# Time mixing: small products on 64x64 tiles, and TensorE's order pinned as written

## The chip, the cores and the metric

The kernel runs on one core of one Trainium2 chip. A core has five engines with a queue each: TensorE (PE, matrix products into PSUM), VectorE (DVE), ScalarE (ACT), GpSimd (POOL) and SyncE (SP, which issues the loads here). The metric is the device time of one execution in microseconds. Three runs of the kernel before took 2772.35, 2776.08 and 2783.49 us; the median is 2776.08.

## The reference

A trunk of two layers over 256 positions of width 2048, in f32. The first layer is RWKV-7 time mixing with 32 heads of 64, followed by a squared-ReLU MLP; the second is banded attention and an MLP. The part that matters is the recurrence of the time mixing:

```python
kk = heads(k * k_k)
kk = kk / jnp.maximum(jnp.sqrt(jnp.sum(kk * kk, axis=-1, keepdims=True)), 1e-12)
k = k * (1 + (a - 1) * k_a)
decay = jnp.exp(-jnp.exp(heads(w_log)))

def step(S, inp):
    r_t, w_t, k_t, v_t, kk_t, a_t = inp
    sa = jnp.einsum('bhvk,bhk->bhv', S, -kk_t)
    S = (S * w_t[:, :, None, :] + sa[..., None] * (kk_t * a_t)[:, :, None, :]
         + v_t[..., None] * k_t[:, :, None, :])
    y = jnp.einsum('bhvk,bhk->bhv', S, r_t)
    return S, y
```

After it `y` is normalized per head, `sum(r*k*r_k)*v` is added, the result is multiplied by a gate `g` and goes through `w_o`.

## The kernel before

Everything is held transposed, channels on the 128 partitions and 256 positions along the row. Two heads fill the partitions, so the 2048 channels are 16 *pairs* (`Pair`). The recurrence is done in 4 chunks of 64 positions: inside a chunk the update by `sa` is a triangular system, which `invert` solves by inverting a 64x64 matrix per head and chunk, doubling the size of the inverted blocks level by level (1, 2, 4, 8, 16, 32).

A pair goes through four stages, which run as generators, one yield a step:

- the projections (`proj_steps` in `layer_a`): k and r of the pair, 2 x 16 units of *large* products. A unit (`proj2`, L394 and L395) multiplies 128 rows by the high half of the weights with 512 columns and by the low half with 256. The weights are split into the halves `wH` (ACT, L360) and `wL` (DVE, L363) in f32r. The generator yields every 2 units, 16 steps.
- `early` (8 steps): decay and learning rate from the LoRA products (L130, L131), the norm of `kk`, the scaled keys `kr`, `bh`, `kh`.
- `invert` (13 calls): the products `gr` of keys per chunk, then the inversion, which ends in `uf` (`u`).
- `late` (16 steps): the chain over chunks (`g`, `sa`, the state `zs`, and `py`, the output), three steps a chunk, then the norm of the output and the gate.

In round `p` of the loop (19 rounds) four pairs are under way: `late` of pair p-3, `invert` of p-2, `early` of p-1, the projections of p. A round has 16 slots. In each slot the three small stages go on by their share of steps, then the projections by one. From round 16 on, products of `w_o` (L383 to L385) stand in for the projections. In some slots one step of the adaLN sums is put in (`ada`: DVE adds a row of weights to `acc`, L423; `ada_sum` reduces `acc` on TensorE, L435).

The order of each engine's queue is chosen at compile time by a scheduler, which plays the program through with estimated durations and takes the earliest traced instruction that is ready. One thing is fixed by hand here: with `issue_after(other[-back])` (L817) the large products of a slot go behind the last small product of the slot before. Apart from that the scheduler may put large products ahead of small ones that aren't ready, and the reverse.

A product of f32 operands runs as two instructions (two passes), each with a weight load of its own. The instruction shapes differ by stage: `each` (L97) takes one 64x64 tile of TensorE per head; `tiles` (L103) works on the 32x32 diagonal or off-diagonal blocks of the inversion, four (two at the last level) side by side; `head_sums` (L120) sums the squares over each head with one 128x128 matrix `bones`, after `parts` (L106 to L116) has split the operand into two f32r halves on ACT and POOL; the large products take 128x128.

The inversion's level `l` in words: `u` holds the inverted 32x32 diagonal blocks, `tt` its 32x32 transposes (DVE, L235), `al` the masked blocks of the matrix (POOL, L239); first product `al`,`tt` into PSUM `iv`, copied to `xs` (ACT, L241); second product `xs`,`u`, added to `u` (DVE, L252). The last level joins the two 32-row halves with `co`, and `uf` collects the result.

Of the kernel before, what the change touches and what calls it, by code (L numbers as in the profile page):

```python
# [36 lines left out]
def _constants():  # L37
# [10 lines left out]
    put("cols", np.tile(np.array([RMS_EPS, GN_EPS, -0.5, 1.0, 1 / 32], np.float32), (P, 1)))  # L48
# [5 lines left out]
    for l in range(5):  # L54
        b = 1 << l
        m = ((i[:, None] // (2 * b) == i[None, :] // (2 * b))
             & (i[:, None] % (2 * b) >= b) & (i[None, :] % (2 * b) < b))
        put(f"lev{l}", np.tile(-m.T[:H, :H].astype(np.float32), (2, 1)))
    put("eye", np.eye(C))
    put("eye_h", np.tile(np.eye(H), (2, 1)))  # L60
    p = np.arange(P)
    bones = (p[:, None] // C == p[None, :] // C).astype(np.float32)
    put("bones", bones)
# [6 lines left out]
QS = [slice(H * i, H * i + H) for i in range(4)]  # L70
C_RMS, C_GN, C_MHALF, C_ONE, C_32ND = range(5)


class Pair:
# [19 lines left out]
    def each(self, o, lhsT, rhs):  # L94
        for c in range(4):
            for K in self.heads:
                self.b.nc.tensor.matmul(o(c)[K], lhsT(c)[K], rhs(c)[K], start=True, stop=True)  # L97

    def tiles(self, o, lhsT, rhs, pairs):

        for c in range(4):
            for R, K in pairs:
                self.b.nc.tensor.matmul(o[QS[K], c, :], lhsT[QS[R], c, :], rhs[QS[R], c, :], start=True, stop=True,  # L103
                                        tile_position=(H * R, H * K))

    def parts(self, func, src, scale=1.0):  # L106

        nc, pw = self.b.nc, self.b.pw
        H, L = (pw.tile([P, T], F32R, tag=n, bufs=2, name=n) for n in ("sH", "sL"))
        nc.scalar.activation(H, src, func, scale=scale)  # L110
        if func != AF.Copy:
            t = self.s("pt", 2)
            nc.scalar.activation(t, src, func, scale=scale)
            src = t
        nc.gpsimd.tensor_tensor(out=L, in0=src, in1=H, op=ALU.subtract)  # L115
        return H, L  # L116

    def head_sums(self, ps, parts):
        for i, t in enumerate(parts):
            self.b.nc.tensor.matmul(ps, self.b.bones, t, start=(i == 0), stop=(i == 1))  # L120

    def early(self):
# [7 lines left out]
        nc.tensor.matmul(z[:, 0:T], lw[:, 0, :], self.tw, start=True, stop=True)  # L130
        nc.tensor.matmul(z[:, T:2 * T], lw[:, 1, :], self.ta, start=True, stop=True)  # L131
# [7 lines left out]
        sq = self.parts(AF.Square, k, vec("k_k", j))  # L139
# [39 lines left out]
        rkp = self.parts(AF.Copy, rkp)  # L179
# [13 lines left out]
    def invert(self):  # L193
        b, nc, s, ch, kr, bk, bh, kh = self.b, self.b.nc, self.s, self.ch, self.kr, self.bk, self.bh, self.kh
        cst, pp = b.cst, b.pp

        def every(name):
            return cst(name).unsqueeze(1).to_broadcast([P, 4, H])

        def half(name, bufs):  # L200
            return b.pw.tile([P, 4, H], F32, tag=name, bufs=bufs, name=name)

# [11 lines left out]


        da, co, u = half("da", 2), half("co", 2), half("u", 2)
        for i, K in enumerate(QS):
            n = H * (i % 2)
            nc.scalar.copy(da[K], pg[K, :, n:n + H])
            if i % 2 == 0:  # L220
                nc.scalar.mul(co[K], pg[K, :, H:C], -1.0)
        nc.gpsimd.tensor_tensor(out=u, in0=da, in1=every("lev0"), op=ALU.mult)
        yield
        nc.vector.tensor_tensor(out=u, in0=u, in1=every("eye_h"), op=ALU.add)
# [6 lines left out]
        uf = self.u = b.uf[self.j % 2]  # L231
        down, up = ((0, 1), (2, 3)), ((1, 0), (3, 2))
        for l in range(1, 6):
            tt_, xs = half("tt", 1), half("xs", 1)
            nc.vector.transpose(out=tt_.rearrange("p c t -> p (c t)"), in_=u.rearrange("p c t -> p (c t)"))  # L235
            pi = pp.tile([P, 16, H], F32, tag="iv", bufs=1, name="iv")[:, 0:4, :]
            if l < 5:
                al = half("al", 2)
                nc.gpsimd.tensor_tensor(out=al, in0=da, in1=every(f"lev{l}"), op=ALU.mult)  # L239
                self.tiles(pi, al, tt_, [(i, i) for i in range(4)])  # L240
                nc.scalar.copy(xs, pi)  # L241
            else:
                self.tiles(pi, co, tt_, down)
                for i, K in enumerate(QS):
                    if i % 2:
                        nc.scalar.copy(xs[K], pi[K])
                    nc.gpsimd.tensor_copy(uf[K, :, H * (i % 2):H * (i % 2) + H], u[K])
            yield
            pi = pp.tile([P, 16, H], F32, tag="iv", bufs=1, name="iv")[:, 0:4, :]
            if l < 5:  # L250
                self.tiles(pi, xs, u, [(i, i) for i in range(4)])
                nc.vector.tensor_tensor(out=u, in0=u, in1=pi, op=ALU.add)  # L252
            else:
                self.tiles(pi, xs, u, up)
                for K in QS[::2]:
                    nc.vector.tensor_copy(uf[K, :, H:C], pi[K])
            if l == 2:
                pg = pp.tile([P, 4, P], F32, tag="gr", bufs=1, name="gr")
                self.each(lambda c: pg[:, c, :], lambda c: ch(kh)[:, c, :], lambda c: kr[:, c, :])
                mk = self.mk = self.big("mk", 2)  # L260
                nc.vector.tensor_tensor(out=mk, in0=pg, in1=ui, op=ALU.mult)
            yield

    def late(self):
# [7 lines left out]
        for c in range(4):  # L272
            pch = pp.tile([P, 3, C], F32, tag="chn", bufs=1, name="chn")
            g, sa = (pw.tile([P, C], F32, tag=n_, bufs=2, name=n_) for n_ in ("g", "sa"))
            for K in heads:
                nc.tensor.matmul(pch[K, 0, :], mk[K, c, 0:C], bk[K, 2, c, :], start=True, stop=(c == 0))  # L276
            if c:
                for K in heads:
                    nc.tensor.matmul(pch[K, 0, :], kr[K, c, 0:C], zs[K, :], start=False, stop=True)
            nc.scalar.copy(g, pch[:, 0, :])  # L280
            yield
            for K in heads:
                nc.tensor.matmul(pch[K, 1, :], u[K, c, :], g[K, :], start=True, stop=True)
            nc.scalar.mul(sa, pch[:, 1, :], -1.0)
            for K in heads:
                nc.tensor.matmul(ch(py)[K, c, :], bk[K, 2, c, :], mk[K, c, C:P], start=True, stop=False)
            if c:
                for K in heads:
                    nc.tensor.matmul(ch(py)[K, c, :], zs[K, :], kr[K, c, C:P], start=False, stop=False)
            yield  # L290
            if c < 3:
                for K in heads:
                    nc.tensor.matmul(pch[K, 2, :], bk[K, 1, c, :], bk[K, 2, c, :], start=True, stop=False)
                for K in heads:
                    nc.tensor.matmul(pch[K, 2, :], bk[K, 0, c, :], sa[K, :], start=False, stop=True)
# [7 lines left out]
            for K in heads:  # L303
                nc.tensor.matmul(ch(py)[K, c, :], sa[K, :], ch(ar)[K, c, :], start=False, stop=True)
# [3 lines left out]
        sq = self.parts(AF.Square, py)  # L308
# [8 lines left out]
        for i in range(2):  # L317
            nc.tensor.matmul(pg, self.lg[:, i, :], self.tg[:, i, :], start=(i == 0), stop=(i == 1))
# [5 lines left out]
class Body:  # L324
# [52 lines left out]
    def proj(self, ps, w, a, kts=(0, KT), first=True, last=True):  # L377

        nc = self.nc
        for kt in range(*kts):  # L380
            H, L = w[kt // HK]
            i = kt % HK
            nc.tensor.matmul(ps, H[:, i, :], a(kt)[:, 0, :], start=(first and kt == 0), stop=False)  # L383
            nc.tensor.matmul(ps, H[:, i, :], a(kt)[:, 1, :], start=False, stop=False)
            ins = nc.tensor.matmul(ps, L[:, i, :], a(kt)[:, 0, :], start=False, stop=(last and kt == KT - 1))  # L385
        return ins.ins

    def proj2(self, ps, w, a, kts=(0, KT)):

        nc = self.nc  # L390
        for kt in range(*kts):
            H, L = w[kt // HK]
            i = kt % HK
            nc.tensor.matmul(ps, H[:, i, :], a(kt), start=(kt == 0), stop=False)  # L394
            ins = nc.tensor.matmul(ps[:, 0, :], L[:, i, :], a(kt)[:, 0, :], start=False, stop=(kt == KT - 1))  # L395
# [34 lines left out]
    def ada_sum(self, acc, dst, half, bias):  # L430
        nc = self.nc
        ps = self.psm()[:, :HK]
        for n in range(HK):
            for g in range(0, P, 32):
                nc.tensor.matmul(ps[g:g + 32, n:n + 1], acc[:, n * P + g:n * P + g + 32], self.col(C_ONE),  # L435
# [19 lines left out]

    def last_pe(self):
        pe = self.nc.tensor.engine
        return next(i for i in reversed(self.nc.cur_bb.bb.instructions) if i.engine == pe)
# [61 lines left out]
    def run(self):  # L520
# [16 lines left out]
        self.lazy, self.fins = False, iter(())  # L537
        self.ada_done = set()
# [40 lines left out]
    def layer_a(self, st, sp):  # L579
# [169 lines left out]
        with ExitStack() as s1:  # L749
# [5 lines left out]
            self.bones = pw.tile([P, P], F32R, name="bones")  # L755
            self.uf = [pw.tile([P, 4, C], F32, name=f"uf_{i}") for i in range(2)]
            nc.scalar.copy(self.bones, self.cst("bones"))
            for e, u in zip(e01, self.uf):
# [69 lines left out]
            self.fin(HK)  # L828
        return v
# [261 lines left out]
```

## Time and profile before

| | |
|---|---|
| runs before | 2772.35, 2776.08, 2783.49 us |
| profiled execution | 2773.6 us |
| its span, granted clock | 2771.8 us, 0.986 |
| first `gr` product | 248.4 us |
| first and last start of `chn` (L276, L283) | 261.2, 752.4 us |
| first and last start of `o` (L383, L385) | 684.1, 780.5 us |

The time mixing's loop over pairs lies between some 222 us (first `pj` unit at 221.7) and 752 us of the span; what stands before it computes v and the adaLN values, what stands behind it is `w_o`, the MLPs and the attention. In rows of the profile, busy time is the union of an engine's instructions; matmuls overlap, so the time a matmul costs is read from one start to the next, not from its duration. A timeline row merges successive instructions of one line: start, length, engine, line, tiles, shape, count. In a row by groups the numbers behind the bar are busy time, the mean of one in ns, the engine's idle time before them and what ended it.

### The profile page before, as it was taken

The page shows a single profiled execution, that of the slowest core. Times are in us where ns is not written, and L with a number is a line of the kernel's source. Part 1 is how long each engine was busy: PE and PEld are TensorE (multiplying, and loading weights), DVE is VectorE, ACT ScalarE, POOL GpSimd, SP SyncE. Part 2 cuts the span into 40 slices and gives each one's busy share as a digit, 9 for nine tenths or more (in the row PEclk, how much of TensorE's full clock was granted, in tenths as well). Part 3 has the DMA queues.
Part 4 walks back from the last instruction along what each step waited for, and adds up shares of the span by engine and source line. Part 5 has one row for each costly group of instructions (what it writes and reads, how often), then busy time and mean ns, then how long its engine had stood idle before and what let it go on. Part 6 is the DMA issues. An engine that isn't in the chain of part 4 may idle for free.

```text
span 2771.8 us, 57644 instructions
## 1 busy us (share of the span) xinstructions
PE 2653.9 (96%) x23402; PEld 2217.6 (80%) x23402; DVE 2087.3 (75%) x3098; ACT 1260.9 (45%) x2214; POOL 301.8 (11%) x416
## 2 busy tenths in 40 slices
PE   6998999999998999999999899999989999999997
PEld 3677777777887888888888788877878888888886
DVE  4568778878889888888788896799786566665665
ACT  2345555556344434344344354465444344443444
POOL 0003443443220000000000200000100000000002
PEclk9999999999999999999999999999999999999999
DMA  9886556555687888888888868888876555555553
GB/s 297 269 281 193 169 171 196 176 176 162 216 302 243 298 308 305 300 314 296 299 306 302 304 218 282 268 293 268 279 242 216 187 186 186 187 183 189 185 188 122
DMA packets 217387, 662.60 MB, mean 239 GB/s; under 512 B 21408, under 2 KB 68896, under 8 KB 217120
## 3 DMA queue, kind: packets, MB, share of 16 engines
q1 hardware_dynamic: 215056, 656.36, 71.5%
q8 instruction: 184, 3.01, 0.4%
q10 hardware_dynamic: 2064, 2.54, 0.3%
q14 instruction: 83, 0.68, 0.1%
HBM read 656.72 MB, written 2.10 MB: 238 GB/s over the span
## 4 chain that ended last, share of the span: by engine, by line
PE 76%; DVE 9%; DMA 7%; issue 4%; POOL 1%; ACT 1%; DVEq 0%; SPq 0%; ACTq 0%; POOLq 0%
PE pj L394 40%; PE pj L395 20%; DMA raw<-w_ada 5%; DVE wL L363 3%; DVE acc L423 2%; PE iv L103 2%; PE gr L97 1%; DMA raw<-w_ada_kv 1%; PE m L625 1%; DVE un L504 1%; PE o L383 1%; PE ms L97 1%; POOL sL L115 1%; PE chn L276 1%; DVE aHL L506 1%
## 5 line engine op out<-in xcount | busy, mean ns | idle before, releaser
L394 PE MATMUL pj<-aHL,wH 128*128 128x512 f32 x3712 | 1353.5, 405 | 26.0 <-DVE aHL L506 22.4
L360 ACT CAST wH<-raw 128x1024 fp32r<-128x1024 f32 x772 | 807.0, 1047 | 949.4 <-PE pj L394 622.1
L363 DVE TENSOR_TENSOR wL<-raw,wH 128x1024 fp32r<-128x1024 f32 x772 | 946.1, 1228 | 290.7 <-ACT wH L360 288.8
L395 PE MATMUL pj<-aHL,wL 128*128 128x256 f32 x3712 | 1049.3, 283 | 7.5 <-DVE wL L363 7.2
L394 PEld LDWEIGHTS pj<-aHL,wH 128*128 128x128 f32 x3712 | 700.3, 189 | 199.2 <-issue 28.0
L394 PE MATMUL pj<-hHL,wH 128*128 128x512 f32 x2048 | 722.0, 397 | 4.5 <-DVE hHL L882 4.5
L395 PEld LDWEIGHTS pj<-aHL,wL 128*128 128x128 f32 x3712 | 705.3, 190 | 14.6 <-DVE wL L363 11.9
L395 PE MATMUL pj<-hHL,wL 128*128 128x256 f32 x2048 | 574.3, 281 | 4.6 <-DVE wL L363 4.5
L423 DVE SCALAR_TENSOR_TENSOR acc<-raw,ct,acc 128x1024 f32<-128x1024 f32 x360 | 470.4, 1307 | 139.8 <-DMA raw<-w_ada 104.0
L394 PEld LDWEIGHTS pj<-hHL,wH 128*128 128x128 f32 x2048 | 384.3, 188 | 97.9 <-DVE hHL L882 6.7
L395 PEld LDWEIGHTS pj<-hHL,wL 128*128 128x128 f32 x2048 | 386.8, 189 | 8.1 <-DVE wL L363 7.7
L482 POOL TENSOR_TENSOR ss<-ss,sq 128x256 f32<-128x256 f32 x56 | 65.0, 1160 | 1599.7 <-ACT sq L481 1599.4
L901 DVE SCALAR_TENSOR_TENSOR x<-pj,mod,x 128x256 f32<-128x256 f32 x256 | 123.1, 481 | 51.7 <-PE pj L395 48.8
L881 ACT CAST hHL<-t 128x256 fp32r<-128x256 f32 x128 | 51.4, 403 | 67.6 <-DVE t L880 67.3
L625 PE MATMUL m<-rawa,crep 128*32 128x256 f32 x512 | 47.4, 449 | 17.5 <-DMA rawa<-w_ada 16.9
L481 ACT ACTIVATE sq<-x 128x256 f32<-128x256 f32 x60 | 25.0, 418 | 70.5 <-DVE x L901 39.6
L880 DVE SCALAR_TENSOR_TENSOR t<-t 128x256 f32<-128x256 f32 x128 | 53.9, 422 | 3.0
L882 DVE TENSOR_TENSOR hHL<-t,hHL 128x256 fp32r<-128x256 f32 x128 | 53.4, 418 | 0.6 <-ACT hHL L881 0.5
L862 DVE TENSOR_TENSOR t<-pj,t 128x256 f32<-128x256 f32 x128 | 53.2, 417 | 0.0
L239 POOL TENSOR_TENSOR al<-da,csts 128x128 f32<-128x128 f32 x64 | 40.7, 647 | 67.4 <-PE iv L103 62.7
L861 ACT COPY t<-pj 128x256 f32<-128x256 f32 x128 | 46.6, 366 | 0.0
L685 PE MATMUL t<-aHL,wH 128*128 128x256 f32 x128 | 38.1, 298 | 5.8 <-DVE v L693 3.6
(230 smaller groups left out, 2483.0 us busy)
## 6 DMA issues: line engine op xcount, KB each, us to landing
raw<-w_ada SPq DMA_DIRECT2D x320, 512.0 KB, 4.7
raw<-w_up SPq DMA_DIRECT2D x256, 512.0 KB, 4.9
raw<-w_down SPq DMA_DIRECT2D x256, 512.0 KB, 4.3
rawa<-w_ada SPq DMA_DIRECT2D x64, 512.0 KB, 6.8
raw<-w_ada_kv SPq DMA_DIRECT2D x64, 512.0 KB, 5.4
raw<-w_k SPq DMA_DIRECT2D x32, 512.0 KB, 4.2
raw<-w_r SPq DMA_DIRECT2D x32, 512.0 KB, 4.7
raw<-w_o SPq DMA_DIRECT2D x32, 512.0 KB, 5.2
```

The costliest lines, as they stand in the source:

```text
L97: self.b.nc.tensor.matmul(o(c)[K], lhsT(c)[K], rhs(c)[K], start=True, stop=True)
L103: self.b.nc.tensor.matmul(o[QS[K], c, :], lhsT[QS[R], c, :], rhs[QS[R], c, :], start=True, stop=True, tile_position=(H * R, H * K))
L360: nc.scalar.copy(Hf, raw)
L363: eng.tensor_tensor(out=Lf, in0=raw, in1=Hf, op=ALU.subtract)
L394: nc.tensor.matmul(ps, H[:, i, :], a(kt), start=(kt == 0), stop=False)
L395: ins = nc.tensor.matmul(ps[:, 0, :], L[:, i, :], a(kt)[:, 0, :], start=False, stop=(kt == KT - 1))
L423: nc.vector.scalar_tensor_tensor(out=acc, in0=raw, scalar=ck, in1=acc, op0=ALU.mult, op1=ALU.add)
L482: (eng or nc.gpsimd).tensor_tensor(out=self.ss, in0=self.ss, in1=sq, op=ALU.add)
L625: nc.tensor.matmul(ps[g:g + 32, part, :W], crep[:, kt, :], raw[:, i, :], start=(part == 1 and kt < 4), stop=(part == 0 and kt >= KT - 4), ...
L880: nc.vector.scalar_tensor_tensor(out=t, in0=t, scalar=0.0, in1=t, op0=ALU.max, op1=ALU.mult)
L882: nc.vector.tensor_tensor(out=h[:, 1, :], in0=t, in1=h[:, 0, :], op=ALU.subtract)
L901: nc.vector.scalar_tensor_tensor(out=x, in0=ps[:, i, :], scalar=self.mods[(layer, 5)][:, n:n + 1], in1=x, op0=ALU.mult, op1=ALU.add)
```

## The change

Three things are changed, all in the pair loop.

1. `tiles` goes. The inversion's products use `each`, so one 64x64 tile per head: the masked matrix has 64 rows and 64 columns a chunk (`level`), the moving operand 32 columns (`tt` or `u`). `xs` is spread to 64 columns by two ACT copies with an even and an odd row mask as scale, and the last level uses two buffers `corner` with zeros in the other half. The first level, elementwise before, becomes a product with `eye_h`.
2. `parts` and `bones` go. `head_sums` takes f32 operands and one 64x64 tile per head.
3. `mm` wraps every product of the loop: while `in_order` is set, the instruction is put behind the one traced before it on TensorE. The loop runs the small stages in every slot and the projections, two steps (4 units), in every second slot; `fin(2)` in every slot becomes `fin(4)` in every second.

```diff
     def each(self, o, lhsT, rhs):
         for c in range(4):
             for K in self.heads:
-                self.b.nc.tensor.matmul(o(c)[K], lhsT(c)[K], rhs(c)[K], start=True, stop=True)
+                self.b.mm(o(c)[K], lhsT(c)[K], rhs(c)[K], start=True, stop=True)
...
+    def head_sums(self, ps, t):
+        for K in self.heads:
+            self.b.mm(ps[K], self.b.cst("ones")[K, 0:C], t[K], start=True, stop=True)
...
+        def level(l):
+            t = s("al", 2)
+            nc.gpsimd.tensor_tensor(out=ch(t), in0=ch(A), in1=cst(f"lev{l}").unsqueeze(1).to_broadcast([P, 4, C]),
+                                    op=ALU.mult)
+            return t
+
+        def product(lhsT, rhs):
+            pi = pp.tile([P, 16, H], F32, tag="iv", bufs=1, name="iv")[:, 0:4, :]
+            self.each(lambda c: pi[:, c, :], lambda c: ch(lhsT)[:, c, :], rhs)
+            return pi
...
+        A = s("da", 2)
+        nc.scalar.copy(ch(A), pg[:, :, 0:C])
+        al = level(0)
+        yield
+        pi = product(al, lambda c: cst("eye_h"))
+        tt = blocks("tt", 1)
+        nc.vector.tensor_tensor(out=tt, in0=pi, in1=eye_h, op=ALU.add)
+        u = turned(tt)
...
         for l in range(1, 6):
             if l < 5:
+                pi = product(level(l), lambda c: tt[:, c, :])
+                xs = s("xs", 1)
+                for i, own in enumerate((even, odd)):
+                    nc.scalar.activation(spread(xs)[:, :, i, :], pi, AF.Copy, scale=own)
...
             yield
+            pi = product(xs, lambda c: u[:, c, :])
             if l < 5:
                 nc.vector.tensor_tensor(out=u, in0=u, in1=pi, op=ALU.add)
+                tt = turned(u)
...
+    def mm(self, *args, **kw):
+        ins = self.nc.tensor.matmul(*args, **kw)
+        return self.tc.keep_in_program_order(ins) if self.in_order else ins
...
-            stages = ((Pair.late, 16), (Pair.invert, 13), (Pair.early, Pair.EARLY), (None, 16))
-            smalls, larges = [], []
+            stages = ((Pair.late, 16), (Pair.invert, 12), (Pair.early, Pair.EARLY), (None, 16))
+            self.in_order = True
...
-                    for gens, own, other, back in ((live, smalls, larges, 0), ([dense], larges, smalls, 2)):
-                        with tc.issue_after(other[-back]) if back and len(other) >= back else nullcontext():
-                            for g in gens:
-                                while g[2] * 16 < g[1] * (slot + 1):
-                                    next(g[0], None)
-                                    g[2] += 1
-                        own.append(self.last_pe())
+                    for g in live + ([dense] if slot % 2 else []):
+                        while g[2] * 16 < g[1] * (slot + 1):
+                            next(g[0], None)
+                            g[2] += 1
                     self.lazy = True
-                    self.fin(2)
+                    if slot % 2:
+                        self.fin(4)
```

More of the change, by code (lines that the diff above doesn't have):

```diff
@@ L1 @@
 import math
-from contextlib import ExitStack, nullcontext
+from contextlib import ExitStack
 import numpy as np
@@ L96, in each @@
             for K in self.heads:
[L97 to L120, printed above, removed]
+                self.b.mm(o(c)[K], lhsT(c)[K], rhs(c)[K], start=True, stop=True)
+    def head_sums(self, ps, t):
+        for K in self.heads:
+            self.b.mm(ps[K], self.b.cst("ones")[K, 0:C], t[K], start=True, stop=True)
     def early(self):
@@ L129, in early @@
         z = b.psm()
-        nc.tensor.matmul(z[:, 0:T], lw[:, 0, :], self.tw, start=True, stop=True)
-        nc.tensor.matmul(z[:, T:2 * T], lw[:, 1, :], self.ta, start=True, stop=True)
+        b.mm(z[:, 0:T], lw[:, 0, :], self.tw, start=True, stop=True)
+        b.mm(z[:, T:2 * T], lw[:, 1, :], self.ta, start=True, stop=True)
         sw, a = s(), s()
@@ L138, in early @@
         yield
-        sq = self.parts(AF.Square, k, vec("k_k", j))
+        sq = s()
+        nc.scalar.activation(sq, k, AF.Square, scale=vec("k_k", j))
         for o in (sw, a):
@@ L194, in invert, with blocks, spread, turned @@
         b, nc, s, ch, kr, bk, bh, kh = self.b, self.b.nc, self.s, self.ch, self.kr, self.bk, self.bh, self.kh
[L195 to L200, printed above, removed]
+        cst, pp, tt = b.cst, b.pp, None
+        def blocks(name, bufs):
             return b.pw.tile([P, 4, H], F32, tag=name, bufs=bufs, name=name)
+        def spread(t):
+            return t.rearrange("p (c i t) -> p c i t", c=4, i=2)
+        def level(l):
[7 more added lines that the diff above has]
+            return pi
+        def turned(t):
+            o = blocks("tt", 1) if t is not tt else blocks("u", 2)
+            nc.vector.transpose(out=o.rearrange("p c t -> p (c t)"), in_=t.rearrange("p c t -> p (c t)"))
+            return o
         ui = cst("ui").unsqueeze(1).to_broadcast([P, 4, P])
@@ L230, in invert @@
         yield
-        uf = self.u = b.uf[self.j % 2]
-        down, up = ((0, 1), (2, 3)), ((1, 0), (3, 2))
+        uf = self.u = s("uf", 2)
+        even, odd = b.col(C_EVEN), b.col(C_ODD)
         for l in range(1, 6):
-            tt_, xs = half("tt", 1), half("xs", 1)
-            nc.vector.transpose(out=tt_.rearrange("p c t -> p (c t)"), in_=u.rearrange("p c t -> p (c t)"))
-            pi = pp.tile([P, 16, H], F32, tag="iv", bufs=1, name="iv")[:, 0:4, :]
             if l < 5:
[L238 to L241, printed above, removed]
-            else:
[L243 to L247, printed above, removed]
+                pi = product(level(l), lambda c: tt[:, c, :])
+                xs = s("xs", 1)
+                for i, own in enumerate((even, odd)):
+                    nc.scalar.activation(spread(xs)[:, :, i, :], pi, AF.Copy, scale=own)
+            else:
+                nc.scalar.activation(spread(b.corner[0])[:, :, 1, :], spread(A)[:, :, 1, :], AF.Copy,
+                                     scale=b.col(C_NEVEN))
+                pi = product(b.corner[0], lambda c: tt[:, c, :])
+                xs = b.corner[1]
+                nc.scalar.copy(spread(xs)[:, :, 0, :], pi)
+                nc.scalar.activation(spread(uf)[:, :, 0, :], u, AF.Copy, scale=even)
             yield
-            pi = pp.tile([P, 16, H], F32, tag="iv", bufs=1, name="iv")[:, 0:4, :]
+            pi = product(xs, lambda c: u[:, c, :])
             if l < 5:
-                self.tiles(pi, xs, u, [(i, i) for i in range(4)])
                 nc.vector.tensor_tensor(out=u, in0=u, in1=pi, op=ALU.add)
+                tt = turned(u)
             else:
-                self.tiles(pi, xs, u, up)
-                for K in QS[::2]:
-                    nc.vector.tensor_copy(uf[K, :, H:C], pi[K])
+                nc.vector.scalar_tensor_tensor(out=spread(uf)[:, :, 1, :], in0=u, scalar=odd, in1=pi,
+                                               op0=ALU.mult, op1=ALU.add)
             if l == 2:
@@ L303, in late @@
             for K in heads:
-                nc.tensor.matmul(ch(py)[K, c, :], sa[K, :], ch(ar)[K, c, :], start=False, stop=True)
+                b.mm(ch(py)[K, c, :], sa[K, :], ch(ar)[K, c, :], start=False, stop=True)
             yield
         var, pg = pyt[:, 1, :], pyt[:, 1, :]
-        sq = self.parts(AF.Square, py)
+        sq = s("sl", 3)
+        nc.scalar.activation(sq, py, AF.Square)
         yield
@@ L317, in late @@
         for i in range(2):
-            nc.tensor.matmul(pg, self.lg[:, i, :], self.tg[:, i, :], start=(i == 0), stop=(i == 1))
+            b.mm(pg, self.lg[:, i, :], self.tg[:, i, :], start=(i == 0), stop=(i == 1))
         nc.vector.scalar_tensor_tensor(out=rg, in0=v, scalar=b.vec("ln_b", j), in1=rg, op0=ALU.add, op1=ALU.add)
@@ L382, in proj @@
             i = kt % HK
-            nc.tensor.matmul(ps, H[:, i, :], a(kt)[:, 0, :], start=(first and kt == 0), stop=False)
-            nc.tensor.matmul(ps, H[:, i, :], a(kt)[:, 1, :], start=False, stop=False)
-            ins = nc.tensor.matmul(ps, L[:, i, :], a(kt)[:, 0, :], start=False, stop=(last and kt == KT - 1))
+            self.mm(ps, H[:, i, :], a(kt)[:, 0, :], start=(first and kt == 0), stop=False)
+            self.mm(ps, H[:, i, :], a(kt)[:, 1, :], start=False, stop=False)
+            ins = self.mm(ps, L[:, i, :], a(kt)[:, 0, :], start=False, stop=(last and kt == KT - 1))
         return ins.ins
@@ L434, in ada_sum @@
             for g in range(0, P, 32):
-                nc.tensor.matmul(ps[g:g + 32, n:n + 1], acc[:, n * P + g:n * P + g + 32], self.col(C_ONE),
+                self.mm(ps[g:g + 32, n:n + 1], acc[:, n * P + g:n * P + g + 32], self.col(C_ONE),
                                  start=True, stop=True, tile_position=(0, g))
@@ L754, in layer_a @@
             e01 = [pw.tile([P, 4, C + 1], F32, name=f"e01_{i}") for i in range(2)]
[L755 to L758, printed above, removed]
+            self.corner = [pw.tile([P, T], F32, name=f"corner_{i}") for i in range(2)]
+            for e, u in zip(e01, self.corner):
                 nc.vector.memset(e[:, :, 0:1], 1.0)
```

45 lines of the change are left out of this document (17 added, 28 removed).

## The prediction

> **What bounds the kernel now.** I read the page first, then the table by stage, then TensorE's own timeline in the time mixing, then the waits. The page:
>
> ```profile
> span 2771.8 us, 57644 instructions
> PE 2653.9 (96%) x23402; PEld 2217.6 (80%) x23402; DVE 2087.3 (75%) x3098; ACT 1260.9 (45%) x2214; POOL 301.8 (11%) x416
> ```
>
> TensorE (PE) is the bound of the whole. The diff touches only the pair loop of the time mixing, so the question is that stage. Its length comes from the view of the tile `gr`, which each of the 16 pairs starts with:
>
> ```profile
> L97 PE MATMUL gr<-kr,bh x256: 269/269/418, 248.4 to 711.7; 64*64 64x128 f32 x128
> ```
>
> From the first to the last of 16 pairs are 463.3 us, 15 intervals: **30.9 us a pair**. I count 15 pairs in the sums. Three windows inside that stretch, 350 to 650 us, summed:
>
> ```profile
> sum 300.00, PE 293.77 PEld 227.00 DVE 240.88 ACT 157.15 POOL 125.52; mean PE 97.92 PEld 75.67 DVE 80.29 ACT 52.38 POOL 41.84
> ```
>
> Busy time in 300 us, and the mean of a window. PE is busy 98% here, DVE 80%. DVE is the next bound, but only at 0.80 x 30.9 = 24.8 us a pair. What TensorE waits for in the stage (window 220 to 684, engine PE; us in total, times, longest):
>
> ```profile
> PE py L120 <- POOL sL L115: 7.7, 4, 2.2
> PE iv L103 <- DVE tt L235: 4.2, 5, 2.0
> ```
>
> These are the two largest: little waiting. The time is issue, and the timeline of TensorE from 480 to 500 us shows what the issue goes to:
>
> ```profile
> 479.74 0.33 PE L276 MATMUL chn<-bk,mk 64*64 64x64 f32 x3
> ...
> 484.17 0.33 PE L293 MATMUL chn<-bk 64*64 64x64 f32 x4
> 484.33 0.28 PE L295 MATMUL chn<-sa,bk 64*64 64x64 f32 x4
> 484.45 0.28 PE L304 MATMUL py<-ar,sa 64*64 64x64 f32 x4
> 484.66 0.50 PE L394 MATMUL pj<-aHL,wH 128*128 128x512 f32 x1
> 485.00 0.28 PE L395 MATMUL pj<-aHL,wL 128*128 128x256 f32 x1
> 485.21 0.45 PE L103 MATMUL iv<-u,xs 32*32 32x32 f32 x32
> 485.60 0.50 PE L394 MATMUL pj<-aHL,wH 128*128 128x512 f32 x1
> 485.94 0.28 PE L395 MATMUL pj<-aHL,wL 128*128 128x256 f32 x1
> ...
> 494.33 0.28 PE L120 MATMUL ms<-sH,bones 128*128 128x256 f32 x1
> 494.44 0.28 PE L120 MATMUL ms<-sL,bones 128*128 128x256 f32 x1
> 494.56 0.39 PE L394 MATMUL pj<-aHL,wH 128*128 128x512 f32 x1
> 494.79 0.28 PE L395 MATMUL pj<-aHL,wL 128*128 128x256 f32 x1
> 494.90 0.40 PE L394 MATMUL pj<-aHL,wH 128*128 128x512 f32 x1
> ...
> 496.92 0.31 PE L435 MATMUL ms<-csts,acc 128*32 128x1 f32 x16
> 497.15 0.33 PE L276 MATMUL chn<-bk,mk 64*64 64x64 f32 x4
> 497.32 1.04 PE L97 MATMUL gr<-kr,bh 64*64 64x128 f32 x16
> 498.29 0.70 PE L130 MATMUL ms<-tw,lw 96*128 96x256 f32 x2
> ...
> 499.84 0.28 PE L395 MATMUL pj<-aHL,wL 128*128 128x256 f32 x1
> ```
>
> Read starts against starts. Inside a run of large products (494.56, 494.79, 494.90) a unit costs 0.23 + 0.11 us. After a change of the tile shape the same L394 takes 0.34 until L395 (484.66 to 485.00), and L395 takes 0.21 until a small product may start (485.00 to 485.21). Four 64x64 instructions cost 0.12 (484.33 to 484.45); the first four after large ones 0.16, the last four before them 0.21. So large to 64x64 and back costs 0.10 + 0.04 + 0.09 + 0.11 = 0.34 us, **0.17 us a switch** of tile shape. Between the first and the last row of these 20 us the shape (128, 96, 64, 32 rows, or 128x32) changes 28 times: 43 switches in 30.9 us, **7.3 us a pair**. That is what the change can take away.
>
> **The change part by part, per pair.**
>
> *Order (gain).* Large units now come in runs of four after two slots of small stages: 8 runs, 16 switches. Early's first step (L130, 96 rows) adds 2, the sums of `acc` (L435) about 1. 19 instead of 43: 24 x 0.17 = **-4.1 us**. Bounds from the same rows: -3.4 if 20 switches go instead of 24, -4.8 at 0.20 a switch (out of a large run 0.09, into one 0.09 + 0.11, without the cheap 0.04).
>
> *Inversion on 64x64 (loss).* Today a product is 32 instructions in eight sets of four side by side: 0.39 us (485.21 to 485.60), of which 0.14 is switching by the numbers above, so 0.25, 0.031 a set. Afterwards it is 16 instructions in eight sets of two. What prices a set? L435 moves one column, not 32, and its four sets take 0.23 less a switch out of 0.09, so 0.035: the same. So the set pays for its weight load of 32 columns, not for the moving columns, and a load of 64 columns costs what the 64x64 rows show, 0.06 for two (0.12 for four): 0.47 a product. Ten products: 10 x 0.22 = 2.2; the new product of level 0 adds 0.47: **+2.7 us**. Lower bound, if moving columns set the price (32 against 64 in L293): 0.25 a product, +0.25 in all. The Trainium skill, "TensorE: Matmul & The Clock Gate", section "LDWEIGHTS (loading the stationary operand)", prices a load by its columns, about P/1.2 ns, and so speaks against this part: 53 ns for 64, as an estimate 0.43 us a product and +2.2 in all, 0.5 below the value I take.
>
> *Head sums (loss).* Three a pair. Two L120 cost 0.11 + 0.12 = 0.23 now. Then four f32 instructions of 256 columns on two tiles side by side: L97 takes 0.97 for eight sets of 128 columns (497.32 to 498.29), 0.12 a set, so 0.24 for 256, two sets 0.48: 3 x 0.25 = **+0.7 us** (+1.9 if the tiles do not overlap). With the split go the waits for `sL`: 7.7 us over 15 pairs, **-0.5 us**.
>
> *Work off TensorE.* ACT loses the second activation of each split and four of six copies out of `gr`, and writes `xs` twice; POOL loses `sL` and `uf` and multiplies 256 columns for a level in place of 128. ACT at 52% and POOL at 42% hide that as long as no product waits behind it, which is the next term.
>
> *Waits of the pinned order (loss).* Today a small product whose operand isn't ready is passed by large units. Pinned, everything on TensorE stands behind it: the other stage's smalls and the four large units. Between the two slots of a couple lies only the rest of the smalls. The durations behind (350 to 650 us):
>
> ```profile
> L423 DVE SCALAR_TENSOR_TENSOR acc<-raw,ct,acc 128x1024 f32<-128x1024 f32 x55 | 72.9, 1326 | 0.1
> L363 DVE TENSOR_TENSOR wL<-raw,wH 128x1024 fp32r<-128x1024 f32 x39 | 52.0, 1334 | 9.0 <-ACT wH L360 8.9
> L239 POOL TENSOR_TENSOR al<-da,csts 128x128 f32<-128x128 f32 x37 | 24.0, 658 | 42.4 <-PE iv L103 37.6 <-PE chn L279 4.7
> L235 DVE STREAM_TRANSPOSE tt<-u 128x128 f32<-128x128 f32 x49 | 14.8, 303 | 0.4
> L252 DVE TENSOR_TENSOR u<-u,iv 128x128 f32<-128x128 f32 x40 | 11.2, 281 | 11.2 <-PE iv L103 10.8
> L241 ACT COPY xs<-iv 128x128 f32<-128x128 f32 x39 | 10.3, 265 | 17.4 <-PE iv L103 17.2
> ```
>
> And two latencies read off the timeline of all engines:
>
> ```profile
> 482.20 0.33 PE L283 MATMUL chn<-g,uf 64*64 64x64 f32 x4
> 482.58 0.23 ACT L284 ACTIVATE sa<-chn 128x64 f32<-128x64 f32 x1 [1.37 <-PE chn L283]
> ...
> 484.74 0.28 DVE L300 SCALAR_TENSOR_TENSOR zs<-zs,pc,chn 128x64 f32<-128x64 f32 x1 [0.91 <-PE chn L295]
> ```
>
> `sa` is there 0.61 us after L283 starts, `zs` 0.69 us after L295 starts (484.33 to 485.02). To a DVE operation comes a queue: L423 and L363 fill (72.9 + 52.0)/300 = 42% of DVE, a newcomer finds half of 1.33 us left: 0.28, with the short operations some 0.36 us. The couples of slots:
> - 0 and 1: `da`, then POOL's level (0.66 for half the columns, I take 0.8) before the first product: about 1.6 us, under Early's L130 and two late groups, 1.2: wait 0.4.
> - 2 and 3, 8 and 9: `zs`, 0.69 + 0.36 against one product and one group, 0.59: 0.45 each.
> - 8 and 9: `xs` by two copies, 0.3 + 2 x 0.265 + 0.1, less what the wait for `zs` covers: 0.3.
> - 4 and 5, 12 and 13: `u` and `tt`, 0.3 + 0.36 + 0.28 + 0.30 + 0.1 = 1.35 against a head sum or 16 small ones and late's group, about 1.0: 0.4 and 0.3.
> - 10 and 11, 12 and 13: `sa` or the square, 0.61 and ACT's queue against 0.59: 0.2 each.
> - behind the four large units (1.4 us) only the tails of DVE's queue: 0.3.
>
> Sum **+3.0 us**. Bounds: 0.5 if DVE and ACT are always free at the right moment, 6 if each DVE step meets a whole 1.33-us operation. I take 3.0, since `zs` and `tt` rows carry most of it.
>
> Net: -4.1 + 2.7 + 0.7 - 0.5 + 3.0 = **+1.8 us a pair**, 15 pairs: +27 us. The profiled execution took 2773.6 us (span 2771.8 and 1.8 around it), which lies 2.5 under the median of 2776.08. Forecast 2773.6 + 27 = **2801 us**. A half per cent, 14 us, is about what a measurement can tell from no change; it is 0.9 us a pair.
>
> **The rivals.**
> - *The waits stay covered, faster.* Waits under 0.3 us a pair (the net without them is -1.2), or 64x64 products at 0.25 with waits up to 2.7. For it: DVE idles 20% and the rows above show few waits today. Against: 80% busy with 1.3-us pieces. With waits at 0 it gives 2773.6 - 18 = 2756; with 0.25 products and waits of 1.2, -2.45 x 15: 2737.
> - *A price by the instruction, faster.* If a product costs by its count, 16 in place of 32 takes 0.13 of today's 0.25: ten save 1.2, the new one costs 0.13, the term falls from +2.7 to -1.1, and +27 less 15 x 3.8 gives 2744. Against it: a set of two 64x64 takes 0.06, one of four 0.031. The Trainium skill, "TensorEngine Tiling (Array Packing)", section "Instruction Overhead", gives some 60 cycles to each matmul whatever its columns; the 32 instructions in 0.39 us here do not bear that out.
> - *DVE's queue rules, much slower.* Waits of 6 us: net +4.8, 2846. It decides where the eight places above wait 0.56 us each on average (4.5 in all).
> - *The terms cancel.* Waits between 0.3 and 2.1 us: within half a per cent.
> - *The pin does nothing*: the order was as good as written. Then of the 28 switches the 5 between 32 and 64 go (8 a pair, -1.3), and +2.7 + 0.7 - 0.5 stay: +1.6, 2798. Against it: 8 runs of four stand nowhere in the 20 us.
>
> **How the numbers follow.** Forecast (waits 2.1 to 4.5, 2787 to 2823) 0.30; much slower 0.18; pin idle 0.05; within half a per cent 0.17; covered waits or cheap loads 0.24; price by count 0.06. So faster 0.30, same 0.17, slower 0.53. Range 2740 to 2852: down to the cheap loads with few waits, up to the full queue and a little over; the likeliest case alone spans 2787 to 2823.
>
> **What would show it.** Right: `gr` 32 to 34 us apart; timeline rows of L394 and L395 in fours; 16 `iv` instructions in about 0.47 us; PE's busy share in the stage below 93% and waits by `zs`, `tt`, `u` and the level at the head of its list; no wait for `sL`. Wrong: 16 `iv` in 0.25 us, waits under 1 us a pair, or DVE above 90% and the pair below 30 us.

## The result, and the profile after

The changed kernel takes 2846.93 us (median of four runs, 2844.55 to 2851.60), the kernel before 2779.53 (four runs): 1.0247 times the time before, with a 95% interval of 1.0219 to 1.0276. That is slower, as forecast, by 67 us; the forecast was 27. It lies in the range on record and almost on the rival "DVE's queue rules", 2846 us. The page after:

```profile
span 2842.8 us, 54118 instructions
PE 2673.3 (94%) x21706; PEld 2250.0 (79%) x21706; DVE 2080.0 (73%) x3082; ACT 1253.6 (44%) x2165; POOL 234.3 (8%) x304
```

The span grew by 71.0 us. The tile `gr` gives the pair's length (all products stand under one line now, that of `mm`, so rows are told apart by tile):

```profile
L340 PE MATMUL gr<-kr,bh x256: 269/269/417, 245.1 to 779.9; 64*64 64x128 f32 x128
```

534.8 us over 15 intervals: 35.65 us a pair against 30.9. 15 x 4.75 = 71 us, so the pair loop holds the whole loss. The windows 350 to 650 us (PE, weight load, DVE, ACT, POOL, then the granted clock, DMA share, GB/s), before and after:

```profile
350.00:450.00 100.00, 96.44 (x1814) 74.85 (x1814) 80.35 (x149) 50.96 (x142) 38.25 (x53) 0.98 0.57 180
450.00:550.00 100.00, 99.62 (x1929) 76.18 (x1929) 80.78 (x154) 52.30 (x147) 41.18 (x55) 1.00 0.57 182
550.00:650.00 100.00, 97.71 (x1856) 75.97 (x1843) 79.76 (x148) 53.88 (x149) 46.09 (x58) 0.98 0.57 179
```

```profile
350.00:450.00 100.00, 89.18 (x1366) 72.82 (x1364) 68.70 (x129) 47.51 (x128) 26.04 (x30) 0.95 0.48 150
450.00:550.00 100.00, 89.35 (x1283) 72.65 (x1284) 67.51 (x124) 42.42 (x116) 27.42 (x28) 0.91 0.49 155
550.00:650.00 100.00, 86.44 (x1291) 70.24 (x1290) 69.18 (x127) 44.63 (x120) 23.12 (x26) 0.95 0.52 163
```

PE falls from 98% to 88% busy, no other engine takes its place (DVE 80% to 68%), and the clock falls from 0.99 to 0.94. What TensorE waited for (220 to 800 us; total, times, longest):

```profile
PE iv L340 <- DVE tt L196: 29.8, 25, 2.4
PE iv L340 <- POOL al L185: 27.5, 16, 2.5
PE iv L340 <- ACT xs L234: 8.6, 16, 1.2
PE chn L340 <- DVE zs L291: 0.7, 2, 0.6
```

With a last row of 0.2 for `zs` these are 66.8 us, 4.2 a pair, nearly all of it in the inversion. The wait for `al` comes once in each of the 16 pairs, at the first level. TensorE's timeline at one of them:

```profile
485.65 0.66 PE L340 MATMUL iv<-u,xs 64*64 64x32 f32 x16
486.14 0.66 PE L340 MATMUL ms<-csts,v 64*64 64x64 f32 x16
486.63 0.60 PE L340 MATMUL py<-sl,csts 64*64 64x256 f32 x4
...
492.99 1.04 PE L340 MATMUL gr<-kr,bh 64*64 64x128 f32 x16
493.96 0.70 PE L340 MATMUL ms<-tw,lw 96*128 96x256 f32 x2
494.50 0.59 PE L340 MATMUL ms<-ta,lw 96*128 96x256 f32 x2
495.02 0.33 PE L340 MATMUL chn<-g,uf 64*64 64x64 f32 x4
495.19 0.28 PE L340 MATMUL py<-mk,bk 64*64 64x64 f32 x4
497.94 1.06 PE L340 MATMUL iv<-csts,al 64*64 64x32 f32 x16 [2.47 <-POOL al L185]
498.81 1.95 PE L340 MATMUL ms<-csts,s 64*64 64x64 f32 x32
500.69 0.79 PE L340 MATMUL pj<-aHL,wH 128*128 128x512 f32 x1
501.29 0.41 PE L340 MATMUL pj<-aHL,wL 128*128 128x256 f32 x1
501.50 0.63 PE L340 MATMUL pj<-aHL,wH 128*128 128x512 f32 x1
501.93 0.41 PE L340 MATMUL pj<-aHL,wL 128*128 128x256 f32 x1
```

Three things stand here. A 64x64 product costs 0.49 us (485.65 to 486.14; 0.47 was forecast). Then TensorE stands idle for 2.47 us (495.47 to 497.94). And behind that TensorE runs at half speed: 32 instructions of `ms` take 1.88 us (498.81 to 500.69), where 16 took 0.49 a little earlier, and of the large units it is 0.21 us from the 256 columns to the next 512 and 0.43 to the next 256 (501.29, 501.50, 501.93), where the rows of before show 0.11 and 0.23. The granted clock in the trace is 0.50 from 496.9 to 503.7 us: it falls inside the gap, 1.45 us after it began. The other engines in that stretch, out of the timeline of all:

```profile
493.60 1.28 DVE L421 SCALAR_TENSOR_TENSOR acc<-raw,ct,acc 128x1024 f32<-128x1024 f32 x1
...
494.79 1.22 DVE L361 TENSOR_TENSOR wL<-raw,wH 128x1024 fp32r<-128x1024 f32 x1
...
496.26 0.41 DVE L209 TENSOR_TENSOR ar<-gr,csts 128x256 f32<-128x256 f32 x1
...
496.71 0.37 ACT L213 COPY da<-gr 128x256 f32<-128x256 f32 x1 [1.08 <-DVE ar L209]
...
497.16 3.08 POOL L185 TENSOR_TENSOR al<-da,csts 128x256 f32<-128x256 f32 x3 [15.46 <-ACT da L213]
```

`gr` is complete at 494.03. ACT's copy `da`, which the level needs, starts only at 496.71, released by DVE's `ar`, and `ar` stood behind two operations of 1.28 and 1.22 us and a short one in DVE's queue. Both read the one PSUM bank of `gr`, and `ar` is traced first. The Trainium skill, "PSUM — Partial Sum Buffer", section "PSUM bank collisions raise a hardware error", has it that two engines must not touch one bank and quadrant at the same time, two reads included, so that their order has to be enforced; this trace is in line with it: `da` starts 0.04 us after the end of `ar`.

### The profile page after: what moved, and what is told of

It is laid out like the page before. It is cut to its first block, busy times and chain, and to the rows that moved or that the text cites. A ratio compares the mean times of both kernels' runs of the same rounds, so it can differ in the third digit from the quotient of the medians.

```text
span 2842.8 us, 54118 instructions
## 1 busy us (share of the span) xinstructions
PE 2673.3 (94%) x21706; PEld 2250.0 (79%) x21706; DVE 2080.0 (73%) x3082; ACT 1253.6 (44%) x2165; POOL 234.3 (8%) x304
## 4 chain that ended last, share of the span: by engine, by line
PE 57%; DMA 6%; DVE 6%; issue 2%; ACT 0%; DVEq 0%; SPq 0%; ACTq 0%
PE pj L340 54%; DMA raw<-w_ada 5%; DVE wL L361 2%; DVE acc L421 1%; DMA raw<-w_ada_kv 1%; PE o L340 1%; DVE x L895 0%; PE pT L980 0%; DVE un L498 0%; PE po L987 0%; PE m L340 0%; DVE aHL L500 0%; PE S L958 0%; PE S L957 0%; ACT wH L358 0%
## 5 line engine op out<-in xcount | busy, mean ns | idle before, releaser
L185 POOL TENSOR_TENSOR al<-da,csts 128x256 f32<-128x256 f32 x80 | 79.2, 1001 | 310.5 <-PE chn L340 136.7
L234 ACT ACTIVATE xs<-iv,csts 128x128 f32<-128x128 f32 x128 | 40.1, 365 | 67.2 <-PE iv L340 67.0
L620 PE MATMUL m<-rawa,crep 128*32 128x256 f32 x512 | 46.4, 440 | 18.5 <-DMA rawa<-w_ada 17.9
L245 DVE TENSOR_TENSOR u<-u,iv 128x128 f32<-128x128 f32 x64 | 18.1, 283 | 56.4 <-PE iv L340 55.8
L340 PE MATMUL iv<-tt,al 64*64 64x32 f32 x1024 | 40.3, 218 | 18.1 <-DVE tt L196 18.1
```

Of the source, the lines that this page charges most:

```text
L185: nc.gpsimd.tensor_tensor(out=ch(t), in0=ch(A), in1=cst(f"lev{l}").unsqueeze(1).to_broadcast([P, 4, C]), op=ALU.mult)
L340: ins = self.nc.tensor.matmul(*args, **kw)
L620: nc.tensor.matmul(ps[g:g + 32, part, :W], crep[:, kt, :], raw[:, i, :], start=(part == 1 and kt < 4), stop=(part == 0 and kt >= KT - 4), ...
```

## The experiments

Theories for the 4.75 us a pair: **waits** (the pinned order lets DVE's queue, and the copy behind `ar`, stop TensorE), **tiles** (the 64x64 products are themselves the loss), **clock** (idle time lowers the clock, which costs beyond the wait). Ratios are to the kernel before, run beside it on the same chip. What each run showed, at a glance; the last four columns are read from the one profiled execution of each, between the first and the last `gr`: the pair's length, TensorE's idle time a pair, the changes of tile shape a pair as counted in the trace, and the time in the whole stretch at a granted clock of 0.50:

| run | ratio (interval) | us a pair | idle a pair | switches a pair | us at half clock |
|---|---|---|---|---|---|
| before | 1 | 30.9 | 0.9 | 42.5 | 10 |
| the change | 1.0247 (1.0219 to 1.0276) | 35.65 | 4.2 | 18.7 | 58 |
| e1 tiles alone | 1.0095 (1.0069 to 1.0121) | 32.8 | 0.5 | 37.0 | 7 |
| e2 pin alone | 1.0176 (1.0152 to 1.0200) | 34.3 | 4.2 | 33.9 | 75 |
| e3 copy first | 1.0148 (1.0124 to 1.0172) | 33.3 | 2.9 | 18.7 | 24 |
| e4 fill the wait | 1.0222 (1.0194 to 1.0250) | 34.9 | 2.8 | 18.7 | 24 |
| e5 = e3, short `acc` | 1.0042 (1.0026 to 1.0059) | 31.8 | 2.0 | 18.7 | 3 |
| e6 = e3, runs of two | 1.0096 (1.0070 to 1.0122) | 33.15 | 1.2 | 31.3 | 34 |
| e8 = e3, invert first | 1.0117 (1.0097 to 1.0137) | 33.0 | 2.2 | 18.7 | 38 |
| e7 head sums alone | 1.0022 (1.0009 to 1.0034) | 31.45 | 0.5 | 45.0 | 7 |
| e10 late's sum alone | 1.0018 (1.0003 to 1.0034) | 30.7 | 0.6 | 43.5 | 3 |
| e12 no `issue_after` | 0.9960 (0.9947 to 0.9972) | 30.6 | 0.7 | 43.5 | 7 |
| e9 groups, not pinned | 0.9949 (0.9936 to 0.9961) | 30.1 | 0.4 | 41.1 | 7 |
| e13 groups of eight | 0.9969 (0.9956 to 0.9982) | 30.35 | 0.9 | 39.0 | 7 |

**The two halves apart.** First the tiles, under the loop of before:

```diff
+                    for gens, own, other, back in ((live, smalls, larges, 0), ([dense], larges, smalls, 2)):
+                        with tc.issue_after(other[-back]) if back and len(other) >= back else nullcontext():
...
-            self.in_order = True
```

> 64x64 tiles and f32 head sums, but the loop and the free order of the kernel before. By the terms on record (products +2.7, head sums +0.7, no wait for sL -0.5, the 32/64 switches -1.3) +1.6 us a pair: about 2800 us. If the 64x64 products themselves are what makes the changed kernel slow, it comes out at 2830 or more; if the pinned order is all of it, at 2780.

2798.3 us, +26. The forecast's terms (+24) hold as a sum. Then the pin and the loop, under the tiles of before:

```diff
-                self.b.nc.tensor.matmul(o(c)[K], lhsT(c)[K], rhs(c)[K], start=True, stop=True)
+                self.b.mm(o(c)[K], lhsT(c)[K], rhs(c)[K], start=True, stop=True)
...
+                    for g in live + ([dense] if slot % 2 else []):
```

> 32x32 tiles and split head sums as before, but the changed loop with TensorE's order pinned. If waits of the pinned order are the loss, 2820 to 2840 us with 3 to 4 us of waits a pair (the switches stay near 43, since each 32x32 product between 64x64 ones costs two). If the tiles are the loss, about 2780.

2819.6 us, 1.76% slower. Its waits:

```profile
PE iv L347 <- DVE tt L235: 56.3, 45, 2.8
PE chn L347 <- DVE zs L300: 2.7, 3, 1.5
```

`tt` alone is 3.5 us a pair. (The switches did not stay near 43: 33.9 are counted.) So the pin with its loop costs about twice what the tiles cost, and the two (0.95 + 1.76) add up to within 0.3% of the change. Tiles as the main loss are ruled out.

**The wait at the first level.** One pair of lines changes places:

```diff
-        ar = self.ar = s("ar", 2)
-        nc.vector.tensor_tensor(out=ch(ar), in0=pg[:, :, C:P], in1=ui[:, :, C:P], op=ALU.mult)
         A = s("da", 2)
         nc.scalar.copy(ch(A), pg[:, :, 0:C])
+        ar = self.ar = s("ar", 2)
+        nc.vector.tensor_tensor(out=ch(ar), in0=pg[:, :, C:P], in1=ui[:, :, C:P], op=ALU.mult)
```

> The changed kernel with one line moved: ACT's copy of gr to da ahead of DVE's product ar on the same PSUM bank. If the wait for the first level comes from the copy standing behind ar in DVE's queue, the 27.5 us of waits for al fall below 10 and the half-clock stretches go with them: 2815 to 2825 us. If POOL's product itself (1.0 us) is the wait, no more than 5 us are gained.

2812.3 us; the ratio falls by 0.0099, some 27 us, for a line moved. The waits after it:

```profile
PE iv L338 <- DVE tt L196: 30.1, 22, 2.6
PE iv L338 <- ACT xs L232: 8.6, 15, 1.2
PE iv L338 <- POOL al L185: 4.7, 12, 1.0
```

22.8 us of waits for `al` are gone, and 2.3 us a pair, 35 us in 15. Some smaller waits grew, so that TensorE's idle time falls by 1.4 us a pair; the rest goes with the clock: 24 us at half speed in place of 58 are up to 1.1 us a pair. The half-speed stretches did not all go, as had been expected.

**The clock by itself.** The wait is kept and TensorE is given work in it:

```diff
-        pi = product(al, lambda c: cst("eye_h"))
+        pi = pp.tile([P, 16, H], F32, tag="iv", bufs=1, name="iv")[:, 0:4, :]
+        for t in (bh, kh, bh, kh, al):
+            self.each(lambda c: pi[:, c, :], lambda c: ch(t)[:, c, :], lambda c: cst("eye_h"))
```

> The changed kernel with four extra products of ready operands (1.9 us of TensorE work, overwritten) ahead of the first level's product, so that TensorE works while it waits. If the half-speed stretches of the clock behind that wait cost time of their own, 2825 to 2835 us, with fewer stretches at half clock; if the waits alone are the loss, 2845 to 2855.

2833.3 us. The clock comes back:

```profile
350.00:450.00 100.00, 95.19 (x1569) 78.63 (x1569) 69.67 (x132) 44.68 (x122) 24.85 (x30) 0.97 0.52 157
450.00:550.00 100.00, 92.97 (x1575) 77.10 (x1575) 74.43 (x133) 47.73 (x128) 28.36 (x30) 1.00 0.54 170
550.00:650.00 100.00, 91.44 (x1497) 75.18 (x1496) 70.03 (x127) 44.95 (x121) 26.24 (x29) 0.97 0.55 169
```

The pair is 0.74 us shorter although it holds 1.9 us of useless products and TensorE's idle time falls by 1.4 us only (the waits for `tt` grew a little), so the half speed that went, 34 of 58 us, had cost about 1.2 us a pair. In the time this is not settled: the ratio, 1.0222, is 0.0025 below the change's, and the intervals overlap.

**DVE's queue.** On top of e3, the `acc` operation in the loop works on 8 of 1024 columns (so it leaves out most of those sums):

```diff
+                    m = 8 if self.in_order else n_
-                    nc.vector.scalar_tensor_tensor(out=acc, in0=raw, scalar=ck, in1=acc, op0=ALU.mult, op1=ALU.add)
+                    nc.vector.scalar_tensor_tensor(out=acc[:, :m], in0=raw[:, :m], scalar=ck, in1=acc[:, :m],
+                                                   op0=ALU.mult, op1=ALU.add)
```

> e3_copy_first with DVE's adaLN accumulation in the loop cut to 8 of its 1024 columns (it leaves out that part of the sums). If the 30 us that TensorE still waits for tt are DVE's queue of 1.3-us operations, they fall below 15 us and the time by 15 to 25 us against e3; if they are the chain u, tt itself, nothing moves.

2786.4 us, 0.0106 below e3, some 29 us, and in the list:

```profile
PE iv L338 <- DVE tt L196: 15.8, 17, 1.2
```

Half of the wait for `tt` is that one operation's queue; the longest wait falls from 2.6 to 1.2 us, by about the length of one `acc`. 15.8 stood just over the line drawn (15), and the time moved more than the waits: the pair is 1.5 us shorter, of which 0.8 is idle time and up to 0.7 the clock (3 us at half speed in place of 24).

**More runs, or another order, in the pinned loop.** e3 with two units after every slot, and e3 with the inversion's step first where a couple of slots holds two:

```diff
-                    for g in live + ([dense] if slot % 2 else []):
+                    for g in live + [dense]:
```

> e3_copy_first with two large units after every slot in place of four after every second: 8 more runs a pair, 16 switches of 0.17 us are +2.7 us a pair (+40 us). Between two steps of the inversion there are then always large units, which take away most of the 43 us of waits for tt, xs and al and the rest of the half-clock stretches (-3 us a pair). Net -0.5 to +1 us a pair against e3, 2805 to 2827 us. If a switch were free, 2770.

```diff
+                    for g in sorted(live, key=lambda g: (g[1] != 12) if slot % 4 == 0 else 0) + ([dense] if slot % 2 else []):
```

> e3_copy_first with the inversion's step put first of the smalls in the first slot of those couples of slots that hold two of its steps. The late group of that slot (0.35 us) then lies between the two. If waits of the pinned order are the loss, the waits for tt and xs (38.7 us) fall by 0.35 us at each of about 50 places that wait, -8 to -15 us; if late then waits in their place for sa and zs, nothing is gained.

e6 takes 2802.3 us: `tt` 17.9 us, `xs` and `al` off the list, the time just under what was expected, the pair 0.17 us shorter. With idle time down by 1.7 us a pair and the clock lower (34 us at half speed in place of 24, up to 0.3), the eight more runs cost some 1.2 us, less than half of the 2.7 expected. They bring 12.6 more switches, not 16, so 0.09 us each. The price is rough: it comes from one profile of each, and the times lie 0.0052 apart, which is more than the pairs show. e6 also tells that pin and groups of four make the waits together: with the pin and two units after every slot 1.2 us of idle time are left. e8 takes 2807.8: `tt` 20.4 and `xs` 1.2, a fall of 17 us where 8 to 15 were expected, but `zs` 5.9 and `sa` 2.4 instead of 1.5 and 1.8. Its gain on e3, 0.003, is within the intervals. There part of the wait moves to `late`; neither order comes to 30.9.

**The head sums.** Alone in the kernel before, and late's alone:

```diff
-        sq = self.parts(AF.Square, k, vec("k_k", j))
+        sq = s()
+        nc.scalar.activation(sq, k, AF.Square, scale=vec("k_k", j))
```

> The kernel before with only the head sums changed (f32, 64x64 tiles, no split). By the terms on record +0.7 - 0.5 = +0.2 us a pair: within 8 us of the kernel before, so that the loss of e1_tiles_alone (26 us) lies in the inversion's products. If the head sums are that loss, 2790 or more.

> The kernel before with late's head sum alone in f32 on 64x64 tiles: its wait for sL (7.7 us in all) goes, one head sum costs 0.25 us more (4 us in all), and where it stands between large units two switches (0.34 us) come: -4 to +2 us.

+0.22% and +0.18%: 6 and 5 us, small losses, with intervals of 2 to 9 and 1 to 9 us. e7 is as expected. e10 lies above its -4 to +2, if its interval just reaches in; its wait for `sL` is gone and its pair, 30.7, no longer than before, so the loop does not show where the 5 us are. What is left of the loss of e1, some 20 us, is the inversion's, by subtraction.

**The grouping without the pin.** The kernel before, one line changed, and its neighbours: groups of eight (`slot % 4 == 3`), and the kernel before without the edge of `issue_after`:

```diff
-                    for gens, own, other, back in ((live, smalls, larges, 0), ([dense], larges, smalls, 2)):
+                    for gens, own, other, back in ((live, smalls, larges, 0), ([dense] if slot % 2 else [], larges, smalls, 2)):
```

> The kernel before (32x32 tiles, order free behind issue_after) with the projections in every second slot, 4 units at once. If grouping alone takes switches away, they fall from 42 to about 35 a pair and the time by 7 x 0.17 x 15 = 18 us, to 2758; if the free order breaks the runs up again, the same as before within 8 us; if waits come with the grouping and not with the pin, 2790 or more.

> e9_group_unpinned with 8 units after every fourth slot. If longer groups go on taking time off, 2750 to 2758 us; if large units are then missing as filler while small products wait, 2770 or more, with waits for tt or wL above 10 us in the stage.

> The kernel before without issue_after, the order wholly the scheduler's. If the hand-made edge costs nothing, the same within 8 us. If it keeps large units from running ahead of the smalls, large units are used up early and the smalls at the end of a round wait: 2785 to 2800.

e9 takes 2763.7 us, 0.5% less than the kernel before and the fastest here; e12 0.4% and e13 0.3% less. None came out as expected: e9 took off 14 us with 41.1 switches where 18 us with 35 were expected, e12, some 11 us below the kernel before, is faster than either outcome named for it, and e13 lies between its two. The runs don't stay whole in e9; where a small product becomes ready it goes in between, even inside a unit:

```profile
483.12 0.39 PE L394 MATMUL pj<-aHL,wH 128*128 128x512 f32 x1
483.43 0.44 PE L103 MATMUL iv<-u,xs 32*32 32x32 f32 x16
483.80 0.39 PE L395 MATMUL pj<-aHL,wL 128*128 128x256 f32 x1
```

So its gain, 0.76 us a pair, does not come from many fewer switches, as was expected. In its one profile 0.5 of it is idle time (0.4 us a pair against 0.9). Why that falls is left open: e12 shows that the edge of `issue_after` costs something by itself, and e9 has half as many of these edges. What e9 does show is that groups of four bring no waits when small products may be overtaken (its largest list entry is 4.2 us, for `sL`); the waits of the change come with the pin.

## Why the prediction was right and wrong

**Direction, stage and kind of loss: right.** PE's idle time by `tt` and the level, runs of four, the vanished wait for `sL`, PE under 93%. The sign came out of the same sum. Two of the signs named did not come: `gr` is 35.65 us apart, not 32 to 34, and `zs` is not at the head of the list.

**Tiles, +2.7, head sums +0.7 - 0.5: right.** 0.49 us a product in the timeline; e1 +26 us against +24 (with 5.5 fewer switches, not 8); e7 +6 us against +3.

**The order's gain, -4.1: the count right, the price probably too high.** The switches fall from 42.5 to 18.7 a pair, 43 to 19 on record, and the step out of a run is 0.21 us again (482.35 to 482.56 in the trace after). But e6 pays 0.09 us a switch; at that price the 24 fewer are worth 2.2 us, not 4.1.

**The step that failed is the waits, +3.0, with the clock that follows them put at nothing.** 4.2 us a pair were measured, and they lay elsewhere:
- Slots 0 and 1: 0.4 was forecast, 27.5/16 = 1.7 measured. The working let `da` start when `gr` was done. It starts behind `ar`, and `ar` behind DVE's queue. The trace of before had the row that says so, with TensorE not yet the one to wait:

```profile
499.91 0.26 ACT L219 COPY da<-gr 32x128 f32<-32x128 f32 x1 [1.57 <-DVE ar L213]
```

- `tt`: 0.7 was forecast, 29.8/16 = 1.9 measured. A newcomer was charged the mean of what is left of one operation, 0.36 us, once for the chain. The single waits reach 2.4: `u` and `tt` each queue anew, here `u` behind `wL` and `tt` behind `acc`, and e5 shows it by taking `acc` away:

```profile
339.92 1.22 DVE L361 TENSOR_TENSOR wL<-raw,wH 128x1024 fp32r<-128x1024 f32 x1
...
341.05 0.28 DVE L245 TENSOR_TENSOR u<-u,iv 128x128 f32<-128x128 f32 x1
...
341.25 1.28 DVE L421 SCALAR_TENSOR_TENSOR acc<-raw,ct,acc 128x1024 f32<-128x1024 f32 x1
...
342.45 0.30 DVE L196 STREAM_TRANSPOSE tt<-u 128x128 f32<-128x128 f32 x1
...
342.90 0.74 PE L340 MATMUL iv<-tt,corner 64*64 64x32 f32 x16 [2.28 <-DVE tt L196]
```

- `xs` was undercharged, 0.3 against 0.5. `zs`, 0.9 against 0.06, and `sa` and the square, 0.4 against nothing, were overcharged.

**A term that was missing: the clock.** From the first to the last `gr` TensorE runs at half clock for 58 us, against 10 before: at most 1.6 us a pair, and e4 measures 1.2 for 34 of these us. The Trainium skill, "TensorE: Matmul & The Clock Gate", section "HAM oscillation — how this bites in real kernels", warns of idle gaps over some 3.4 us; here the clock fell 1.45 us into a gap of 2.47, so shorter gaps were enough.

**The sum again.** TensorE's idle time rose by 3.3 us a pair (0.9 to 4.2), where -0.5 + 3.0 = 2.5 had been forecast. With the tiles' 2.7, the head sums' 0.7 and the clock's 1.2 to 1.6 that is 7.9 to 8.3 us without the order's gain. The 4.75 seen leave 3.1 to 3.5 for it, between e6's 2.2 and the 4.1 on record; its size stays open within these bounds. So of the 3 us a pair that the forecast missed, the clock is the largest part, the waits are about 0.8, and the rest is the order's gain.

The rival that came true in number, "DVE's queue rules", did so by luck: it put the waits at 6 us, and 4.2 were measured; the clock, which it doesn't have, made up much of the difference.

## What to carry to other kernels

Pinning the order of TensorE, the engine that is the bound here, turned latencies of the others into its idle time; groups of four by the order of tracing alone, with ready work free to overtake, did not (e9). Before a wait is priced from the operation's duration, look up what released that operation in the trace of before, on its own engine and on the PSUM bank that it reads; a queue of long operations is met once for each step of a chain. And an idle TensorE can cost twice: the gap, and a stretch at half speed behind it.

## What the runs showed of the hardware

- The granted clock fell to 0.50 inside a wait of 2.47 us, 1.45 us after its start, and stayed there for 6.8 us. Not each wait does it: seven of the 16 waits for `al` come with such a fall (inside or up to 1.8 us behind), and the one of 2.30 us that ends at 572.9 does not. What decides is not shown. Filling the wait with products of no use makes the pair 0.74 us shorter (e4).
- A 64x64 f32 product with 32 moving columns costs 0.49 us for 16 instructions, as much as one with 64 columns (486.14 to 486.63, `ms`): 0.06 a set of two with 32 or 64 columns. With 128 columns (`gr`, 492.99 to 493.96) a set costs 0.12. So from 32 to 64 the moving columns do not set the price.
- Setting aside the clock, a change of tile shape costs 0.09 us by e6 and 0.17 by the starts in the timeline of before; the two are not reconciled.
